# Extra TensorE products with an unread result at three places of a two-layer encoder step, and PSUM buffers dealt out anew in the state-space mixer

## The chip, the cores and the metric

The kernel runs on one core of one Trainium2 chip. The metric is the time of one execution in device microseconds; lower is better. The five engines are named as the profile names them: PE (TensorE's products; PEld is its weight loads), DVE (VectorE), ACT (ScalarE), POOL (GpSimd) and SP (SyncE, which issues most transfers).

## The reference

One inference step of a two-layer encoder over 1024 prompt positions and 64 sample positions, width 1024. Layer 0 mixes with windowed attention, layer 1 with a diagonal state-space model; each layer ends in a gated feed-forward part with a short convolution, and RMS norms stand before and after every part.

```python
def s5_mixer(h, ...):                       # layer 1, 64 groups of 16 channels, 64 complex states each
    lr, li, bbr, bbi = s5_discretize(lam_re, lam_im, log_dt, b_re, b_im)
    ...
        xr = jnp.einsum('blgi,gpi->blgp', u_blk, bbr)
        xi = jnp.einsum('blgi,gpi->blgp', u_blk, bbi)
        ...
        _, _, sr, si = lax.associative_scan(_affine_combine, (ar, ai, xr, xi), axis=1)
        y = jnp.einsum('blgp,gip->blgi', sr, cr) - jnp.einsum('blgp,gip->blgi', si, ci)
    ...
    y = ... + d_skip * h
    z = jax.nn.gelu(y)
    ag = z @ w_glu + b_glu
    return ag[..., :D_MODEL] * jax.nn.sigmoid(ag[..., D_MODEL:]), hr, hi

for i in range(DEPTH):
    x = x + rms_norm(mixer_i(rms_norm(x, g_pre_mix[i])), g_post_mix[i])
    x = x + rms_norm(conv_ffn(rms_norm(x, g_pre_ffn[i])), g_post_ffn[i])
```

## The kernel before

Activations lie with channels on the partitions; the 1088 positions are cut in three blocks (`BLK`: 384, 384 and 320). A big product is done in three passes of fp32r (`mm3`, lines 218 to 222): high part of the weights by low part of the input, high by high, low by high. Weights come one unit of 128x1024 at a time through SP's queue, ACT rounds the high part (L214) and DVE subtracts it (L215).

**The head.** The core starts by loading `x` and the first weight units; `pre_norm` (L281) scales and splits each block on ACT (L288) and DVE (L294), and the first products (L220 to L222, from `attention`) follow as the pieces come. The identity matrix `ident` is made by DVE at L71 in the constructor.

**The norms ahead of the state-space mixer.** When the last block of layer 0's feed-forward part is done, `post_norm` finishes it: sums of squares by products with a column of ones (L254), a root and its reciprocal in a few short DVE steps, the result spread over the partitions by three transposes (L272), then multiplications and additions on DVE (L316, L319). Then `ssm_norm` (L1133) does the same for the norm ahead of the mixer: squares on ACT (L242), sums on DVE (L244, L248), products with ones (L254), the short steps again, and three small products with a selection matrix (L1157). Meanwhile `ssm_bounce` (L1099) writes the block to DRAM and `ssm_load` (L1161) reads it back in another layout as `U`.

**The rounds.** `ssm` (L1179) handles 32 pairs of groups (`q`), 137 columns each (8 positions folded into the rows). `batch` (L1220) takes one or two pairs at a time: 0; 1; then two by two up to 29; 30; 31. These 18 batches run as three stages that overlap (`staged`, L146; the older batch's stage comes first in the program):

- stage 1: TensorE makes the inputs of the scan in the PSUM tile `p1` (L1251, 4 products of 64 weight columns a pair); DVE multiplies them by tables (L1252 and L1255, both read `p1`) and adds (L1256); ACT prepares the tables `sc` and `rd` (L1231, L1234);
- stage 2: DVE scans (L1270) and multiplies by the tables (L1273 makes `gc`, L1274 makes `gs`); ACT copies final states (L1277);
- stage 3: for each pair two PSUM tiles `p3`, `e` = 0 and 1. Each takes one product with the input (L1284, on `U` and `pm`) and four with `gc` and `gs` (L1289, on 64 of the 128 rows: `e` = 0 the upper half, `e` = 1 the lower); ACT copies the two tiles out (L1293). Every fourth pair the copies go to DRAM and come back (L1296, L1301), and ACT applies GELU (L1309, L1312) and rounds (L1318); DVE subtracts (L1322).

All the products named in these stages have plain fp32 operands; the trace shows two records for one such product. The tables `pm` come from DRAM through SP's queue, two transfers a batch of two (L1195). PSUM has eight banks; in this stage they are dealt out as `p1` 2 x 2 banks and `p3` 4 x 1.

After the rounds the gated linear unit begins (`tile_`, L1360), its first product at L220 on `pb`.

**What sets the order.** The program is written for all engines in one sequence; a scheduler reorders it at compile time by its own estimate, and each engine runs its instructions in that fixed order, waiting on semaphores. `order(x, first)` (L112) adds an edge which only the scheduler sees: x is not put before first. A tile pool with a `tag` and `bufs` makes a tile wait for the last reader of the tile that had its buffer.

Of the kernel before, what the change touches and what calls it, by code (L numbers as in the profile page):

```python
# [8 lines left out]
F32 = mybir.dt.float32  # L9
# [6 lines left out]
P = 128  # L16
# [21 lines left out]
NC_ = 137  # L38
# [5 lines left out]
class Core:  # L44
# [173 lines left out]
    def mm3(self, out, w, sl, xh, xl, start, stop):  # L218
# [2 lines left out]
        nc.tensor.matmul(out, w[:, 0, sl], xh, start=False, stop=False)  # L221
        self.last_mm = nc.tensor.matmul(out, w[:, 1, sl], xh, start=False, stop=stop)  # L222


    def rstd(self, src, n, tag, root, bcast=True, first=False, alt=None, adder=None, fine=False):
        nc = self.nc
        adder = adder or nc.vector
        acc = None
        for q in range(4):
            sq = self.n2(n, tag)  # L230
            xq = src[:, 2 * q:2 * q + 2]
            if fine and q == 3:

                adder.tensor_add(acc[:, 0], acc[:, 0], acc[:, 1])
                for j in range(2):
                    nc.scalar.activation(sq[:, j], xq[:, j], AF.Square)
                    adder.tensor_add(acc[:, 0], acc[:, 0], sq[:, j])
                break
            if first:
                nc.gpsimd.tensor_mul(sq, xq, xq)  # L240
            else:
                self.sq[q] = nc.scalar.activation(sq, xq, AF.Square)  # L242
            if q:
                adder.tensor_add(acc, acc, sq)  # L244
            else:
                acc = sq
        else:
            adder.tensor_add(acc[:, 0], acc[:, 0], acc[:, 1])  # L248
        cuts = [min(c, n - P) for c in range(0, n, P)]
        nt = len(cuts)  # L250
        pr = self.sm_ps("pr", int(tag == "sqb") if alt is None else alt)
        st = pr[:, 384:384 + nt]
        for i, c in enumerate(cuts):
            nc.tensor.matmul(st[:, i:i + 1], acc[:, 0, c:c + P], self.ones, start=True, stop=True)  # L254
        v = self.small.tile([P, 4, 4], F32, name="nv" + tag, bufs=3)
        x, hx, r, t = (v[:, i, :nt] for i in range(4))
        if root:
            nc.scalar.activation(x, st, AF.Sqrt, bias=self.eps)
            nc.vector.tensor_scalar(hx, st, 1e-6, -0.5, op0=ALU.add, op1=ALU.mult)
            nc.vector.reciprocal(r, x)  # L260
            self.refine(r, t, hx)
        else:

            nc.vector.tensor_scalar(x, st, 1e-6, None, op0=ALU.add)
            ri = r.bitcast(I32)
            nc.vector.tensor_scalar(ri, x.bitcast(I32), 1, None, op0=ALU.logical_shift_right)
            nc.vector.tensor_scalar(hx, x, -0.5, None, op0=ALU.mult)
            nc.vector.tensor_scalar(ri, ri, -1.0, float(MAGIC), op0=ALU.mult, op1=ALU.add)
            for _ in range(3):
                self.refine(r, t, hx)  # L270
        for i, c in enumerate(cuts if bcast else []):
            nc.tensor.transpose(pr[:, c:c + P], r[:, i:i + 1].to_broadcast([P, P]), self.ident)  # L272
        return pr, r

    def refine(self, r, t, hx):
# [857 lines left out]
    def ssm_norm(self, xt, b):  # L1133

        nc = self.nc
        n = BLK[b][1]
        ps, r = self.rstd(xt, n, "sqa" if b == 2 else "sqb", True, bcast=b < 2, alt=1 - b % 2, adder=nc.gpsimd if b == 0 else None)
        if b == 0:
            jp = self.t4([P, P], "jp", I32)
# [14 lines left out]
        for i, c in enumerate(range(0, n, P)):  # L1154
            c = min(c, n - P) // 8
# [23 lines left out]
    def ssm(self, after):  # L1179
# [4 lines left out]
        with tc.tile_pool(name="ss", bufs=1) as sp:  # L1184
# [2 lines left out]
            self.close_ps()  # L1187
            ps_ctx = tc.tile_pool(name="ps2", bufs=1, space=bass.MemoryType.PSUM)
            ps = ps_ctx.__enter__()

            def load(t, after=None):

# [27 lines left out]
            def batch(qs):  # L1220
# [22 lines left out]
                wk = sp.tile([P, 2, n, 2, 138], F32, name="wk", bufs=3)  # L1243
                A, G = wk[:, 0], wk[:, 1]
                nc.gpsimd.memset(A[:, :, :, 0:1], 0.0)
                p1 = ps.tile([P, 2, 512], F32, name="p1", bufs=2)[:, 0:n, 0:2 * NC_].rearrange("p e (c k) -> p e c k", c=2)
                for i, q in enumerate(qs):
                    for c in range(2):
                        for e, r in enumerate(ROWS):
# [28 lines left out]
                fins.append(x)  # L1278
                yield
                for i, q in enumerate(qs):  # L1280
                    p3 = [ps.tile([P, 512], F32, name="p3", bufs=4)[:, :NC_] for _ in range(2)]
                    for e in range(2):
                        o = OKT + P * e
                        nc.tensor.matmul(p3[e], pm[:, i, o:o + P], U(2 * q + e), start=True, stop=False)  # L1284
                    for c in range(2):
                        for s, g_ in enumerate((gc, gs)):
                            for e, r in enumerate(ROWS):
                                o = OC + P * (c ^ s)
                                nc.tensor.matmul(p3[e], pm[r, i, o:o + P], g_[r, i, c, 0:NC_], start=False, stop=c == 1 and s == 1)  # L1289
                    if q % 4 == 0:  # L1290
                        ys[0] = self.t4([P, 8, NC_], "ys")
                    for e in range(2):
                        out[0] = nc.scalar.activation(ys[0][:, 2 * (q % 4) + e], p3[e], AF.Copy)  # L1293
# [160 lines left out]
def build(tc, a):  # L1454
    nc = tc.nc
    with ExitStack() as ctx:
# [7 lines left out]
        with c.boundary():  # L1464
# [3 lines left out]
            for b in range(3):  # L1468
                step = 2 if b == 0 else 4
                for k in range(0, KD, step):  # L1470
# [4 lines left out]
                    if (b, k) in ((0, 0), (0, 6), (1, 0)):  # L1475
                        c.load_ahead(1 + len(c.ready))
                        c.order(c.loaded, last)
                        last = c.loaded
            c.rest_of_pp()
            for b in range(3):  # L1480
                h.append(c.pre_norm(xt[b], b, g(0), rb, first=b == 0))
# [65 lines left out]
```

## Time and profile before

| | |
|---|---|
| time before, median of 3 runs | 2285.5 us (2285.21 to 2285.83) |
| the profiled execution | 2279.22 us |
| its span, first to last instruction | 2277.4 us |
| PE busy | 2203.5 us (97%) |
| DVE busy | 1683.8 us (74%) |
| ACT busy | 1020.5 us (45%) |
| mean granted clock of TensorE | 0.982 |

A busy share is the time in which the engine had an instruction under way. Matmuls overlap, so the time from one's start to the next one's start tells more than its own length. The granted clock is TensorE's share of 2.4 GHz: 1.00, or 0.50 (1.2 GHz); a value between is a mean over a stretch that has both. In a timeline a line is: start, length, engine, line of the kernel, operation, output and inputs, shapes, count, and in brackets how long the engine sat idle before it and what ended that.

### The profile page before, as it was taken

The numbers are of one execution on the slowest core, as the hardware profiler recorded it, in microseconds if no ns is written. First come the engines' busy times: TensorE is split into PE (matmuls) and PEld (weight loads), VectorE is DVE, ScalarE is ACT, GpSimd is POOL, SyncE is SP. The second block draws the span as 40 slices with busy tenths as digits, with TensorE's granted clock in tenths as the row PEclk, the third lists the DMA queues.
The fourth block names the chain that finished last, engine by engine and source line by source line (L and its number), as shares of the span: only waits on it lengthen the run. The fifth ranks groups of instructions, "written<-read, shape, count | busy, mean of one in ns | idle before, by whom it ended". The sixth has DMA issues, their size and how long they took to land. (4 is left out here: it accounts for less than half of the span.)

```text
span 2277.4 us, 35917 instructions
## 1 busy us (share of the span) xinstructions
PE 2203.5 (97%) x13791; PEld 2126.7 (93%) x13791; DVE 1683.8 (74%) x2954; ACT 1020.5 (45%) x1867; POOL 420.5 (18%) x474
## 2 busy tenths in 40 slices
PE   8999999999999999999978999999999999999997
PEld 7987789999999999999966799999999999999997
DVE  8677648989878776767757845587997787776764
ACT  5255746422333332555544631263444344355543
POOL 6222004100133314001100025452010111110000
PEclk9999999999999999999987889999999999999998
DMA  5100015655245665887749868751265667578773
GB/s 194 36 22 28 20 61 168 236 199 207 91 148 179 194 198 179 278 270 235 241 169 313 227 226 306 277 165 64 95 215 204 239 249 282 183 247 298 230 252 103
DMA packets 208123, 428.46 MB, mean 188 GB/s; under 512 B 23312, under 2 KB 114224, under 8 KB 205008
## 3 DMA queue, kind: packets, MB, share of 16 engines
q1 hardware_dynamic: 175648, 326.56, 43.8%
q0 software_dynamic: 23984, 95.12, 11.5%
q10 hardware_dynamic: 8320, 4.49, 0.8%
q8 instruction: 108, 1.77, 0.3%
q14 instruction: 63, 0.52, 0.1%
HBM read 297.75 MB, written 128.37 MB: 187 GB/s over the span
## 5 line engine op out<-in xcount | busy, mean ns | idle before, releaser
L220 PE MATMUL mm<-hl,whl 128*128 128x384 f32 (+1 forms) x1960 | 645.3, 330 | 15.4 <-ACT whl L214 7.3
L221 PE MATMUL mm<-hh,whl 128*128 128x384 f32 (+1 forms) x1960 | 643.4, 328 | 0.0
L222 PE MATMUL mm<-hh,whl 128*128 128x384 f32 (+1 forms) x1960 | 642.1, 328 | 0.6 <-DVE whl L215 0.6
L220 PEld LDWEIGHTS mm<-hl,whl 128*128 128x128 f32 x1960 | 369.4, 189 | 19.7 <-ACT whl L214 7.3
L214 ACT ACTIVATE whl<-raw 128x1024 fp32r<-128x1024 f32 x202 | 213.0, 1058 | 356.9 <-PE mm L222 157.4
L222 PEld LDWEIGHTS mm<-hh,whl 128*128 128x128 f32 x1960 | 369.1, 188 | 1.4 <-DVE whl L215 1.4
L221 PEld LDWEIGHTS mm<-hh,whl 128*128 128x128 f32 x1960 | 369.5, 189 | 0.0
L215 DVE TENSOR_TENSOR whl<-raw,whl 128x1024 fp32r<-128x1024 f32 x202 | 252.4, 1254 | 105.8 <-ACT whl L214 105.5
L220 PE MATMUL mm<-gt,whl 128*128 128x384 f32 (+1 forms) x968 | 317.0, 328 | 4.0 <-ACT whl L214 1.5
L222 PE MATMUL mm<-gt,whl 128*128 128x384 f32 (+1 forms) x968 | 315.8, 327 | 0.7 <-DVE whl L215 0.7
L221 PE MATMUL mm<-gt,whl 128*128 128x384 f32 (+1 forms) x968 | 316.0, 327 | 0.0
L220 PEld LDWEIGHTS mm<-gt,whl 128*128 128x128 f32 x968 | 181.7, 188 | 5.5 <-ACT whl L214 1.8
L222 PEld LDWEIGHTS mm<-gt,whl 128*128 128x128 f32 x968 | 181.6, 188 | 1.2 <-DVE whl L215 1.2
L221 PEld LDWEIGHTS mm<-gt,whl 128*128 128x128 f32 x968 | 181.7, 188 | 0.0
L194 DVE TENSOR_TENSOR whl<-raw,whl 128x1024 fp32r<-128x1024 f32 x84 | 94.8, 1135 | 69.3 <-ACT whl L193 68.6
L193 ACT ACTIVATE whl<-raw 128x1024 fp32r<-128x1024 f32 x84 | 82.7, 986 | 123.0 <-DMA raw<-sd 56.2
L407 ACT ACTIVATE t<-u,ppt 128x1090 f32<-128x1090 f32 x88 | 114.2, 1298 | 49.3 <-DVE u L509 22.6
L408 DVE SCALAR_TENSOR_TENSOR t<-u,ppt,t 128x1090 f32<-128x1090 f32 x88 | 123.7, 1408 | 9.3 <-ACT t L407 8.7
L409 DVE SCALAR_TENSOR_TENSOR t<-u,ppt,t 128x1090 f32<-128x1090 f32 x88 | 123.5, 1405 | 0.4
L399 DVE TENSOR_TENSOR u<-rb,mm 128x384 f32<-128x384 f32 (+1 forms) x164 | 80.5, 504 | 21.1 <-PE mm L222 16.4
L551 DVE TENSOR_TENSOR gt<-gr,gt 128x768 fp32r<-128x768 f32 (+2 forms) x106 | 90.4, 882 | 6.0 <-ACT gt L550 5.5
L319 POOL TENSOR_TENSOR y<-y,xl 128x768 f32<-128x768 f32 (+1 forms) x16 | 30.6, 1912 | 347.0 <-DVE y L316 283.7
(384 smaller groups left out, 4194.8 us busy)
## 6 DMA issues: line engine op xcount, KB each, us to landing
raw<-in_w_up SPq DMA_DIRECT2D x88, 512.0 KB, 4.2
raw<-in_w_down SPq DMA_DIRECT2D x74, 512.0 KB, 4.5
raw<-sd SPq DMA_DIRECT2D x40, 512.0 KB, 4.3
sj<-in_w_up POOLq DMA_DIRECT2D x68, 256.0 KB, 5.9
su<-sj POOLq DMA_DIRECT2D x34, 512.0 KB, 5.5
raw<-su SPq DMA_DIRECT2D x34, 512.0 KB, 5.0
pm<-prm SPq DMA_DIRECT2D x32, 522.0 KB, 7.1
gr<-td SPq DMA_DIRECT2D x40, 384.0 KB, 5.4
```

The source lines that it names most:

```text
L193: nc.scalar.activation(w[:, 0], raw, AF.Copy)
L194: nc.vector.tensor_sub(w[:, 1], raw, w[:, 0].bitcast(F32))
L214: nc.scalar.activation(w[:, 0], raw, AF.Copy)
L215: nc.vector.tensor_sub(w[:, 1], raw, w[:, 0].bitcast(F32))
L220: nc.tensor.matmul(out, w[:, 0, sl], xl, start=start, stop=False)
L221: nc.tensor.matmul(out, w[:, 0, sl], xh, start=False, stop=False)
L222: self.last_mm = nc.tensor.matmul(out, w[:, 1, sl], xh, start=False, stop=stop)
L399: nc.vector.tensor_mul(u[:, t0 + 2:t0 + 2 + np_], rb[:, t0:t0 + np_], ps[:, :np_])
L407: nc.scalar.activation(t, u[:, 0:T + 2], AF.Identity, bias=cb(m), scale=cw(0, m))
L408: nc.vector.scalar_tensor_tensor(t, u[:, 1:T + 3], cw(1, m), t, op0=ALU.mult, op1=ALU.add)
L409: self.last_conv = nc.vector.scalar_tensor_tensor(t, u[:, 2:T + 4], cw(2, m), t, op0=ALU.mult, op1=ALU.add)
L551: nc.vector.tensor_sub(x[:, 1, u], raw, x[:, 0, u].bitcast(F32))
```

## The change

A new helper `fill` issues products with the identity as weights into a PSUM tile that nothing reads. It is called at three places: at the head, 14 products of 128 columns, as soon as `ident` is there; in `ssm_norm` for the last block, 7 products of 512 columns, put after the last transpose of the `post_norm` before it; and in stage 3 of each of the 18 batches, one product of 384 columns, put after the two L1284 of the batch's first pair and before its first L1289. The moving operand of the wider ones is a part of the constants `pp` that lies in SBUF. To free a bank for the rounds' tile `idle`, `p1` goes from two buffers (2 banks each) to one, and `p3` from four to five.

```diff
--- before.py
+++ after.py
@@ -221,6 +221,15 @@
         nc.tensor.matmul(out, w[:, 0, sl], xh, start=False, stop=False)
         self.last_mm = nc.tensor.matmul(out, w[:, 1, sl], xh, start=False, stop=stop)
 
+    def fill(self, ps, n, cols, first=None):
+
+        for _ in range(n):
+            x = self.nc.tensor.matmul(ps[:, :cols], self.ident, self.pp[:, 64:64 + cols] if cols > P else self.ident[:, :cols], start=True, stop=True)
+            if first is not None:
+                self.order(x, first)
+            first = x
+        return x
+
 
     def rstd(self, src, n, tag, root, bcast=True, first=False, alt=None, adder=None, fine=False):
         nc = self.nc
@@ -269,7 +278,7 @@
             for _ in range(3):
                 self.refine(r, t, hx)
         for i, c in enumerate(cuts if bcast else []):
-            nc.tensor.transpose(pr[:, c:c + P], r[:, i:i + 1].to_broadcast([P, P]), self.ident)
+            self.last_tr = nc.tensor.transpose(pr[:, c:c + P], r[:, i:i + 1].to_broadcast([P, P]), self.ident)
         return pr, r
 
     def refine(self, r, t, hx):
@@ -1134,6 +1143,8 @@
 
         nc = self.nc
         n = BLK[b][1]
+        if b == 2:
+            self.fill(self.mm_ps("idle"), 7, 512, self.last_tr)
         ps, r = self.rstd(xt, n, "sqa" if b == 2 else "sqb", True, bcast=b < 2, alt=1 - b % 2, adder=nc.gpsimd if b == 0 else None)
         if b == 0:
             jp = self.t4([P, P], "jp", I32)
@@ -1187,6 +1198,7 @@
             self.close_ps()
             ps_ctx = tc.tile_pool(name="ps2", bufs=1, space=bass.MemoryType.PSUM)
             ps = ps_ctx.__enter__()
+            idle = ps.tile([P, 512], F32, name="idle")
 
             def load(t, after=None):
 
@@ -1243,7 +1255,7 @@
                 wk = sp.tile([P, 2, n, 2, 138], F32, name="wk", bufs=3)
                 A, G = wk[:, 0], wk[:, 1]
                 nc.gpsimd.memset(A[:, :, :, 0:1], 0.0)
-                p1 = ps.tile([P, 2, 512], F32, name="p1", bufs=2)[:, 0:n, 0:2 * NC_].rearrange("p e (c k) -> p e c k", c=2)
+                p1 = ps.tile([P, 2, 512], F32, name="p1", bufs=1)[:, 0:n, 0:2 * NC_].rearrange("p e (c k) -> p e c k", c=2)
                 for i, q in enumerate(qs):
                     for c in range(2):
                         for e, r in enumerate(ROWS):
@@ -1278,15 +1290,19 @@
                 fins.append(x)
                 yield
                 for i, q in enumerate(qs):
-                    p3 = [ps.tile([P, 512], F32, name="p3", bufs=4)[:, :NC_] for _ in range(2)]
+                    p3 = [ps.tile([P, 512], F32, name="p3", bufs=5)[:, :NC_] for _ in range(2)]
                     for e in range(2):
                         o = OKT + P * e
-                        nc.tensor.matmul(p3[e], pm[:, i, o:o + P], U(2 * q + e), start=True, stop=False)
+                        x = nc.tensor.matmul(p3[e], pm[:, i, o:o + P], U(2 * q + e), start=True, stop=False)
+                    f = self.fill(idle, 1, 384, x) if i == 0 else None
                     for c in range(2):
                         for s, g_ in enumerate((gc, gs)):
                             for e, r in enumerate(ROWS):
                                 o = OC + P * (c ^ s)
-                                nc.tensor.matmul(p3[e], pm[r, i, o:o + P], g_[r, i, c, 0:NC_], start=False, stop=c == 1 and s == 1)
+                                x = nc.tensor.matmul(p3[e], pm[r, i, o:o + P], g_[r, i, c, 0:NC_], start=False, stop=c == 1 and s == 1)
+                                if f is not None:
+                                    self.order(x, f)
+                                    f = None
                     if q % 4 == 0:
                         ys[0] = self.t4([P, 8, NC_], "ys")
                     for e in range(2):
@@ -1476,6 +1492,7 @@
                         c.load_ahead(1 + len(c.ready))
                         c.order(c.loaded, last)
                         last = c.loaded
+            c.fill(c.mm_ps("idle"), 14, P)
             c.rest_of_pp()
             for b in range(3):
                 h.append(c.pre_norm(xt[b], b, g(0), rb, first=b == 0))
```

## Rows read from the trace of the kernel before

**Rows 1.** The page's first table: busy time of each engine, share of the span, instructions.

```profile
PE 2203.5 (97%) x13791; PEld 2126.7 (93%) x13791; DVE 1683.8 (74%) x2954; ACT 1020.5 (45%) x1867; POOL 420.5 (18%) x474
```

**Rows 2.** Stretches of the span, cut where the granted clock changes: start and end in us, length, busy time and count of PE, PEld, DVE, ACT, POOL, then the granted clock, the DMA share and GB/s. The last line is all that follows.

```profile
1183.00:1204.00 21.00, 8.55 (x45) 6.92 (x47) 12.49 (x26) 9.77 (x21) 1.36 (x9) 0.51 0.89 317
...
1214.20:1221.00 6.80, 5.75 (x38) 4.66 (x38) 5.10 (x7) 3.74 (x14) 0.23 (x2) 0.50 1.02 394
1221.00:1241.50 20.50, 17.01 (x195) 13.93 (x194) 18.10 (x25) 12.79 (x41) 1.37 (x9) 1.00 0.89 287
1241.50:1255.20 13.70, 13.70 (x68) 11.18 (x68) 7.61 (x13) 4.95 (x12) 0.66 (x2) 0.50 0.71 224
...
1285.90:1296.10 10.20, 9.59 (x42) 8.06 (x42) 4.53 (x7) 3.06 (x16) 0.29 (x2) 0.50 0.75 237
...
1313.20:1326.90 13.70, 13.00 (x51) 11.15 (x51) 5.59 (x9) 7.10 (x13) 3.40 (x5) 0.50 0.63 186
1326.90:2277.00 950.10, 929.91 (x5638) 924.98 (x5636) 686.62 (x1008) 401.43 (x613) 166.94 (x217) 0.99 0.63 214
```

**Rows 3.** Timeline of DVE in the rounds: starts of L1252, and the L1322 that belongs to every second batch.

```profile
1204.88 0.73 DVE L1252 TENSOR_TENSOR wk<-pm,p 128x548 f32<-128x548 f32 x1 [1.76 <-PE p L1251]
...
1221.70 0.73 DVE L1252 TENSOR_TENSOR wk<-pm,p 128x548 f32<-128x548 f32 x1 [2.23 <-PE p L1251]
...
1227.02 0.72 DVE L1252 TENSOR_TENSOR wk<-pm,p 128x548 f32<-128x548 f32 x1
...
1232.08 0.72 DVE L1252 TENSOR_TENSOR wk<-pm,p 128x548 f32<-128x548 f32 x1
...
1241.61 1.42 DVE L1322 TENSOR_TENSOR zl<-z,zh 128x384 fp32r<-128x384 f32 x3
...
1253.86 0.73 DVE L1252 TENSOR_TENSOR wk<-pm,p 128x548 f32<-128x548 f32 x1 [6.09 <-PE p L1251]
...
1295.75 0.72 DVE L1252 TENSOR_TENSOR wk<-pm,p 128x548 f32<-128x548 f32 x1 [5.47 <-PE p L1289]
```

**Rows 4.** Timeline of PE in the rounds and at the start of the gated linear unit, some of its lines.

```profile
1217.62 1.28 PE L1284 MATMUL p<-U,pm 128*128 128x137 f32 x4
1218.83 2.20 PE L1289 MATMUL p<-wk,pm 64*128 64x137 f32 x16
...
1223.39 0.73 PE L1284 MATMUL p<-U,pm 128*128 128x137 f32 x4
1224.06 1.20 PE L1289 MATMUL p<-wk,pm 64*128 64x137 f32 x16
1225.19 1.62 PE L1251 MATMUL p<-U,pm 128*64 128x137 f32 x24
...
1240.93 0.50 PE L1284 MATMUL p<-U,pm 128*128 128x137 f32 x2 [3.17 <-ACT ys L1293]
...
1246.23 1.28 PE L1284 MATMUL p<-U,pm 128*128 128x137 f32 x4
...
1285.14 0.69 PE L1251 MATMUL p<-U,pm 128*64 128x137 f32 x8 [2.00 <-DMA pm<-prm]
...
1312.49 0.50 PE L1284 MATMUL p<-U,pm 128*128 128x137 f32 x2 [1.94 <-DVE wk L1273]
...
1322.84 0.69 PE L220 MATMUL pb<-zl,whl 128*128 128x384 f32 x1 [0.70 <-ACT ys L1293]
```

**Rows 5.** Timeline of PE in layer 0's feed-forward part: a plain fp32 product of 128 columns (L1050, two records) and an fp32r product of 320 columns by turns.

```profile
653.26 0.38 PE L1050 MATMUL kps<-ct,bd 128*128 128x128 f32 x2
653.40 0.39 PE L221 MATMUL mm<-hh,whl 128*128 128x320 f32 x1
653.62 0.38 PE L1050 MATMUL kps<-ct,bd 128*128 128x128 f32 x2
```

**Rows 6.** Timeline of the head: DVE's identity, the first product, two of the last at the slow pace and two of the first at the fast one, and the place where PE waits for a weight unit that DVE splits.

```profile
1.09 0.23 DVE L71 TENSOR_SCALAR ident<-jp 128x128 f32<-128x128 int32 x1 [0.21 <-POOL jp L97]
...
7.34 0.69 PE L220 MATMUL mm<-hl,whl 128*128 128x384 f32 x1 [7.34 <-ACT whl L214]
...
11.79 0.52 PE L221 MATMUL mm<-hh,whl 128*128 128x384 f32 x1
...
12.11 0.52 PE L222 MATMUL mm<-hh,whl 128*128 128x384 f32 x1
...
12.74 0.34 PE L221 MATMUL mm<-hh,whl 128*128 128x384 f32 x1
...
12.92 0.34 PE L222 MATMUL mm<-hh,whl 128*128 128x384 f32 x1
...
16.52 0.44 PE L222 MATMUL mm<-hh,whl 128*128 128x384 f32 x1 [0.33 <-DVE whl L215]
```

**Rows 7.** Timeline of PE in the norms ahead of the mixer, up to the first product of the rounds.

```profile
1180.87 0.80 PE L254 MATMUL pr<-ones,sqa 128*128 128x1 f32 x6 [1.70 <-DVE sqa L237]
...
1182.89 0.54 PE L272 MATMUL pr<-ident,nvsqa 128*128 128x128 f32 x3 [1.22 <-DVE nvsqa L279]
...
1193.63 1.44 PE L254 MATMUL pr<-ones,sqa 128*128 128x1 f32 x6 [10.20 <-DVE sqa L248]
...
1196.63 1.46 PE L1157 MATMUL pr<-sel 128*128 128x16 f32 x6 [1.56 <-DVE sel L1156]
...
1198.78 1.18 PE L1251 MATMUL p<-U,pm 128*64 128x137 f32 x8 [0.68 <-PE pr L1157]
```

## The prediction

> **What bounds the kernel now.** I read the page's table of engines first: PE is busy in 2203.5 of 2277.4 us [rows 1], so nearly everywhere else the products themselves are the limit and a change can only matter where PE waits or runs slowly. The windows then show where that is [rows 2]: between 1183 and 1327 us the granted clock alternates between 1.00 and 0.50, with half-clock stretches of 21.0, 6.8, 13.7, 10.2 and 13.7 us. These are the norms ahead of the state-space mixer, its rounds, and the first products of the gated unit. After 1326.9 us PE is busy 929.9 of 950.1 us, so what is gained or lost before passes on to the end.
>
> In the rounds, DVE's and PE's timelines are read against each other. At full clock DVE hardly waits: it is busy 18.1 of the 20.5 us from 1221 to 1241.5 [rows 2], and a round of two pairs takes 1232.08 - 1227.02 = 5.06 us of it, plus 1.42 us of L1322 in every second round [rows 3]. At half clock DVE waits for PE: 1.76 us at 1204.88, then 2.23, 6.09 and 5.47 [rows 3]. What PE did before each fall is in its own timeline [rows 4]: it idled 3.17 us before 1240.93 behind ACT, which had not yet copied the `p3` tiles out, and 2.00 us before 1285.14 behind a transfer of `pm`.
>
> **The price of a product that nobody reads.** The trace has none of 384 fp32 columns. The nearest row is L1050, 128 fp32 columns between fp32r products of 320: two of its records and one of the other take 653.62 - 653.26 = 0.36 us, of which the other's share is 0.15 (320/384 of the 0.18 us from one fp32r start to the next, 12.74 to 12.92) [rows 5, 6]. So one such product of 128 columns costs 0.21 us, one of 384 by its columns 0.63, one of 512 0.84. From below, two fp32r records of 384 columns are 0.36 us; from above, L1284 takes 0.67 us for two products of 137 columns (1223.39 to 1224.06) [rows 4], 384/137 of one is 0.94. I take 0.7, near L1050, whose weights are also 128 wide. At half clock L1284 takes 1.21 (1217.62 to 1218.83), 1.8 times as long [rows 4], so 1.26.
>
> **The change part by part, as differences to the span.**
>
> *Head: 0.* The 14 products can start at 1.32, when `ident` is done [rows 6], and cost 14 x 0.21 = 2.9 us at full, 5.3 at half pace. They end by about 7 us, where the first real one starts (7.34); from above, by L1284's price, 14 x 0.31 x 1.8 = 7.9, they would hold it 1.9 us. The real products run 0.32 us apart up to 12.4 and 0.18 after it. A faster pace from 7.34 gains nothing: at 16.52 PE waits for DVE's split of a weight unit [rows 6], and DVE waits for no product before it. That wait also hides a delay of 1.9. If it were gone, the 5.1 us at the slow pace would be worth 5.1 x (1 - 0.18/0.32) = 2.2.
>
> *Norms: -0.6.* The clock falls near 1183 after PE has had only 0.80 and 0.54 us of work since 1179 [rows 7], all before the seven products start at 1183.43; so their beginning is at half pace. They take 7 x 0.84 = 5.9 us at full and 10.6 at half, ending between 1189.3 and 1194.0; the real L254 comes at 1193.63. If the clock is up there, L254 takes 0.80, as at 1180.87, for 1.44: -0.64. L1157 (1.46) could save as much again, but PE idles between, as it did before the fall at 1183. Bounds: -1.3, and +5.6 if all seven cost L1284's upper price at half pace (15.8 us, to 1199.2, past L1157's start at 1196.63 and L1251's at 1198.78).
>
> *Start of the rounds: +0.7.* From 1198.78 to 1204.88 PE works without a gap at half clock [rows 3, 7] and DVE waits. Two products of `fill` now stand in this chain. At full clock the 6.1 us become 3.4 + 1.4 = 4.8: -1.3. At half: +2.5. PE is nearly idle from 1195.1 to 1196.6, so half is likelier; but the clock rises within it, and DVE may be given other work.
>
> *Falls in the rounds: -8.0.* The `fill` stands after the first pair's L1284, where PE next waits for `gc` and `gs`. That helps where PE lacked operands (before 1214), less where L1284 itself is held by `p3`, or L1251 by `pm`: `fill` is behind the stall. What it does in every case is to bind the order. At 1240.93 PE made one `p3` tile's five products and then the other's, 5.30 us for a pair; with both L1284 first, as at 1217.62, 3.4 (half clock), because the products on the two halves of the rows run together [rows 4]. So a fall should last shorter. I count the 2.23 us as gone and half of 6.09 and 5.47: -8.0. Bounds 0 and -13.8.
>
> *Tail: -3.4.* From 1312.49 PE needs 10.35 us at half clock for the last two pairs until the gated unit starts at 1322.84 [rows 4]. With the bound order and two `fill` it is 2 x 3.4 + 2 x 1.26 = 9.3 at half, 2 x 1.80 + 1.4 = 5.0 at full; I take -2.5, a little under the middle. The first 4.06 us of the gated unit, to 1326.9, would be 0.18/0.32 of that at full clock: -1.8, half counted.
>
> *Work added: +1.5.* Eighteen times 0.7 is 12.6 us of PE. A warm round has 16/24 of 1.62 for L1251, twice 1.80 and 0.7: 5.4 us, against DVE's 5.06 and, with L1322, 6.5 [rows 3, 4]. The excess of 0.3 shows in some eight rounds without L1322 (2.4, less what the bound order saves); without DVE as cover all 12.6 would count.
>
> *One `p1` buffer: +1.0.* The next batch's L1251 now waits for L1255 of the present one. Until the next L1252 DVE still has the rest of its 5.06 us, some 3.7 us (5.06 less two of 0.72), for PE's 1.1. Behind the waiting L1251 stand later L1284, and ACT waits for those. The fifth `p3` tile lets one L1284 start early. Bounds 0 and +20 (below).
>
> Sum: 0 - 0.6 + 0.7 - 8.0 - 3.4 + 1.5 + 1.0 = -8.8. It is made on the profiled execution (2279.22, 1.8 above its span, 6.3 under the median); the median shown, 2285.5, becomes **2276.7**.
>
> **The rivals.**
>
> *The clock never falls in the rounds (13%).* For it: warm rounds are nearly full, 5.4 of about 5.8 us. Against: the two stalls lie ahead of `fill`. It gives -0.6 - 1.3 - 13.8 - 5.4 - 1.8 + 2.5 = -20.4: 2265.
>
> *The falls stay as they are (17%).* For it: the stalls of 3.17 and 2.00 us are not touched, and with one `p1` PE can't use them for products of a second batch ahead, as it does at 1225.19 (24 records, a batch and a half). Five `fill` at half pace cost 6.3, four pairs no longer made one tile after the other give back 4 x 1.9 = 7.6, the rest +2.6: 2287, about the same. The Trainium skill, "TensorE: Matmul & The Clock Gate", section "A second HAM failure mode: psum-queue depth-cycling", says that small idles between groups of products, while PE goes round its PSUM banks, keep the clock changing; by that rule a buffer less speaks for this case. The trace agrees as far as the stall before 1240.93 is one for a PSUM tile.
>
> *Slower, by the single `p1` (15%).* If L1251 of the next batch ends after L1274 of the present one, its 1.1 us and a handover of 0.2 come on DVE's path in each of some 16 rounds: up to +20, less 10 for half of the first rival's gain, so 2296. It decides when PE stands behind the present batch's two pairs (3.6 + 0.7 us) at the moment L1255 ends: 3.7 us are left then. Against: these pairs' first products can run earlier. The same page, "Step-by-step: what each phase is for", says that products keep their program order, so that a `fill` ahead would delay L1251; no row here shows one overtaken.
>
> **How the numbers follow.** The main case holds 55%, with 2270 to 2283 as its own range. A measurement of this kernel can tell about 0.2%, 4.6 us. Faster by more: nine tenths of the main case, the first rival, a little of the second, 0.64. Same: 0.19. Slower: 0.17. The range 2262 to 2291 leaves out the far ends of the first and third rival.
>
> **What would show it.** Right: between 1204 and 1327 the half-clock stretches shrink from 6.8 + 13.7 + 10.2 + 13.7 = 44.4 us to under 30, L1289 comes in sixteens at a batch's first pair, and DVE's wait of L1252 for PE falls by about 8 us; the head's 16.52 stays. Wrong: `fill` far from 0.7 us, falls at the same places and as long, L1252 waiting in every round for L1251, or L254 held up by the seven.

## The result, and the profile after

The changed kernel took 2268.99 us at the median of its first four runs (2268.03 to 2273.37) against 2285.36 us of the kernel before: a ratio of 0.9936 (95% interval 0.9918 to 0.9953). Twelve more runs on another occasion (e6_again below) gave 0.9975 (0.9961 to 0.9989). It is faster, by 0.25 to 0.65%; the predicted 2276.7 us lies between the two medians, 2269.0 and 2280.0.

The profiled execution took 2268.03 us, span 2266.3; it is the fastest of the four. PE's row of the page, for the one in [rows 1]:

```profile
PE 2199.2 (97%) x13869; PEld 2119.5 (94%) x13869; DVE 1687.6 (74%) x2954; ACT 1021.7 (45%) x1867; POOL 417.5 (18%) x474
```

The windows, cut where the clock changes, columns as in [rows 2]:

```profile
1193.50:1203.50 10.00, 7.75 (x31) 6.46 (x32) 2.59 (x12) 3.10 (x11) 1.17 (x8) 0.50 1.04 392
1210.50:1214.00 3.50, 3.50 (x34) 3.25 (x32) 2.98 (x4) 3.02 (x10) 0.21 (x2) 0.52 1.03 400
1241.00:1244.50 3.50, 3.50 (x26) 3.00 (x28) 1.79 (x3) 1.34 (x7) 0.00 (x0) 0.52 0.56 209
1268.50:1272.00 3.50, 3.50 (x20) 2.17 (x19) 2.83 (x4) 0.13 (x1) 0.00 (x0) 0.52 1.03 407
1272.00:1313.00 41.00, 34.16 (x354) 26.19 (x353) 34.38 (x52) 31.54 (x84) 2.09 (x11) 1.00 0.76 230
1313.00:1316.50 3.50, 3.17 (x10) 3.17 (x11) 2.58 (x5) 1.23 (x3) 1.66 (x3) 0.53 0.64 178
```

Where the kernel before had half clock for 6.8, 13.7, 10.2 and 13.7 us [rows 2], this one has four falls of about 3.4. (The products' lines move: L254 is now L263, L1157 L1168, L1251 L1263, L1252 L1264, L1273 and L1274 L1285 and L1286, L1284 L1296, L1289 L1302, L1293 L1309, L1309 L1325; L227 is the product of `fill`.) PE's timeline of the rounds:

```profile
1226.01 0.81 PE L227 MATMUL idle<-ppt,ident 128*128 128x384 f32 x2
1226.75 1.21 PE L1302 MATMUL p<-wk,pm 64*128 64x137 f32 x16
...
1239.75 0.50 PE L1296 MATMUL p<-U,pm 128*128 128x137 f32 x2 [3.15 <-ACT ys L1309]
1240.09 0.81 PE L227 MATMUL idle<-ppt,ident 128*128 128x384 f32 x2
...
1268.02 0.50 PE L1296 MATMUL p<-U,pm 128*128 128x137 f32 x2 [3.29 <-ACT ys L1309]
1268.36 1.36 PE L227 MATMUL idle<-ppt,ident 128*128 128x384 f32 x2
1269.64 2.20 PE L1302 MATMUL p<-wk,pm 64*128 64x137 f32 x16
...
1311.43 1.36 PE L1302 MATMUL p<-wk,pm 64*128 64x137 f32 x16 [2.22 <-DVE wk L1285]
1313.33 0.69 PE L220 MATMUL pb<-zl,whl 128*128 128x384 f32 x1 [0.54 <-ACT ys L1309]
```

L1302 comes in sixteens, both `p3` tiles by turns (in two batches as 4 and 28 records). The wait for ACT ahead of L1296 is still there, 3.15 and 3.29 us, and the clock still falls behind it. DVE's waits for PE are of the old kind, only shorter (2.23, 6.09 and 5.47 in [rows 3], 13.8 us together; 0.86, 3.42 and 3.68 here, 8.0), and at the start there is one of 4.39:

```profile
1205.03 0.44 DVE L1264 TENSOR_TENSOR wk<-pm,p 128x274 f32<-128x274 f32 x1 [4.39 <-PE p L1263]
...
1210.81 0.72 DVE L1267 TENSOR_TENSOR wk<-sc,p 128x548 f32<-128x548 f32 x1 [0.56 <-ACT sc L1243]
...
1246.54 0.72 DVE L1264 TENSOR_TENSOR wk<-pm,p 128x548 f32<-128x548 f32 x1 [3.68 <-PE p L1263]
...
1259.01 0.72 DVE L1264 TENSOR_TENSOR wk<-pm,p 128x548 f32<-128x548 f32 x1 [0.86 <-PE p L1263]
...
1274.82 0.73 DVE L1264 TENSOR_TENSOR wk<-pm,p 128x548 f32<-128x548 f32 x1 [3.42 <-PE p L1263]
...
1311.32 0.45 DVE L1286 TENSOR_TENSOR wk<-wk,sc 128x276 f32<-128x276 f32 x1
```

**Where the 11.1 us of the spans came from.** I cut both profiles at four events. The norms' first product is 0.15 us earlier (1180.72 for 1180.87 in [rows 7]); from there to the first product of the rounds both take 17.91 (1198.63 and 1198.78). From that product to the end of DVE's last multiplication (L1286 above, L1274 below) the time falls from 114.88 to 113.14 us, -1.7. From there to the gated unit's first product it falls from 9.18 to 1.56, -7.6; what comes after the gated unit begins gives the last 1.6. So the largest piece is the tail. Here is its beginning in the kernel before, whose gated unit starts at 1322.84 [rows 4]:

```profile
1313.22 0.44 DVE L1274 TENSOR_TENSOR wk<-wk,sc 128x276 f32<-128x276 f32 x1
```

Counted on PE in program order, the kernel before has 48 L1289 (six pairs) behind the last L1251, the changed one 16 (two pairs). With two `p1` the scheduler runs stage 1 ahead to the end of the rounds and stage 3 stays behind; with one it can't. Runs of the same letter on PE, A for L1251, B for L1284, C for L1289, F for `fill`, counts behind them:

```
before: ... A7 B2 C8 B2 C8 B1 C1 B1 C7 B1 C1 B1 C7 B1 C4 B1 C4 B1 C1 B1 C7
after:  ... A8 B2 F1 C8 B2 C8 A4 B2 F1 B3 C16 A4 B1 F1 C8 B2 F1 C8
```

`B1 C4 B1 C4` is one `p3` tile and then the other; the kernel before has this in five pairs (from 1240.93, 1263.78, 1272.01, 1286.52 and 1312.49), the changed one in none. Such a pair is dearer at full clock too: the second of them takes 3.11 us (to 1266.89), one by turns 1.80 (1226.82 to 1228.62).

Four of the six pairs were done at 1310.55. PE then stood still until 1312.49, and the last two pairs made the tail. The profile names L1273 for this wait [rows 4], but L1284 reads nothing of L1273; the weight load of the same product names ACT, which had a GELU and a rounding (from 1308.82 on) ahead of the copies that free `p3`:

```profile
1312.14 0.47 ACT L1293 ACTIVATE ys<-p 128x137 f32<-128x137 f32 x2
```

```profile
1312.49 0.30 PEld L1284 LDWEIGHTS p<-U,pm 128*128 128x128 f32 x2 [2.15 <-ACT ys L1293]
```

In the changed kernel one pair is left there (1311.43). The clock is not what shortens the tail: in e6_again, the same program profiled once more, it took 2.38 us, all of them at half clock:

```profile
1323.54:1325.92 2.38, 1.87 (x17) 1.55 (x15) 2.33 (x5) 1.91 (x9) 0.00 (x0) 0.50 0.14 17
```

### The profile page after: what moved, and what is told of

It is laid out like the page before. It is cut to its first block, busy times and chain, and to the rows that moved or that the text cites. A ratio compares the mean times of both kernels' runs of the same rounds, so it can differ in the third digit from the quotient of the medians.

```text
span 2266.3 us, 36080 instructions
## 1 busy us (share of the span) xinstructions
PE 2199.2 (97%) x13869; PEld 2119.5 (94%) x13869; DVE 1687.6 (74%) x2954; ACT 1021.7 (45%) x1867; POOL 417.5 (18%) x474
## 5 line engine op out<-in xcount | busy, mean ns | idle before, releaser
L215 DVE TENSOR_TENSOR whl<-raw,whl 128x1024 fp32r<-128x1024 f32 x202 | 254.9, 1266 | 95.3 <-ACT whl L214 95.1
L559 ACT ACTIVATE gt<-gr 128x768 fp32r<-128x768 f32 (+2 forms) x106 | 78.3, 772 | 38.3 <-DMA gr<-gd 25.6
```

The lines of the kernel that those rows point to most:

```text
L215: nc.vector.tensor_sub(w[:, 1], raw, w[:, 0].bitcast(F32))
```

## The experiments

Theory A: the order that the product binds (both L1296 ahead of the first L1302) does it. Theory B: the product's own work keeps the clock. Theory C: the single `p1` does it. A rival to all: the products at the head and in the norms. What each run showed, by the same cuts (the last four columns are of one profile each; "rounds" and its clock run from 12 us after the first L1251 to the gated unit, "longest" is the longest half-clock stretch that begins in it, "DVE" the time from the first L1251 to the end of the last L1274, "tail" from there to the gated unit):

| kernel | p1/p3, bound, columns | median (runs) | ratio, 95% | rounds, clock | longest | DVE | tail |
|---|---|---|---|---|---|---|---|
| before | 2/4, no, none | 2282.9 to 2285.4 | 1 | 112.06, 0.82 | 13.7 | 114.9 | 9.2 |
| changed | 1/5, yes, 384 | 2269.0 (4) | 0.9936 (0.9918-0.9953) | 102.70, 0.95 | 3.4 | 113.1 | 1.6 |
| e6_again | the same | 2280.0 (12) | 0.9975 (0.9961-0.9989) | 109.80, 0.89 | 10.2 | 119.4 | 2.4 |
| e1_rounds | 1/5, yes, 384, no ends | 2273.9 (10) | 0.9965 (0.995-0.9981) | 105.01, 0.94 | 6.8 | 114.6 | 2.4 |
| e12_rounds | the same | 2276.9 (12) | 0.9969 (0.9956-0.9983) | 106.81, 0.92 | 6.8 | 117.2 | 1.6 |
| e5_small | 1/5, yes, 16, no ends | 2275.7 (10) | 0.9977 (0.996-0.9995) | 108.27, 0.86 | 6.8 | 117.6 | 2.7 |
| e11_sixteen | the same | 2280.1 (12) | 0.9981 (0.9965-0.9997) | 108.64, 0.86 | 6.8 | 118.0 | 2.7 |
| e10_two | 1/5, yes, 2 x 512, no ends | 2281.6 (12) | 0.9988 (0.9972-1.0003) | 108.30, 1.00 | none | 117.5 | 2.8 |
| e9_bound | 2/4, yes, none | 2279.4 (12) | 0.9979 (0.9965-0.9992) | 109.17, 0.86 | 6.8 | 112.8 | 8.4 |
| e3_deal | 1/5, no, none | 2285.3 (10) | 1.001 (0.9991-1.0028) | 109.48, 0.87 | 13.7 | 118.7 | 2.7 |
| e4_ends | 2/4, no, ends only | 2284.2 (10) | 1.0001 (0.9983-1.0019) | 121.54, 0.77 | 34.1 | 120.4 | 13.1 |
| e7_ahead | 1/5, yes, 384 ahead | 2275.4 (12) | 0.9958 (0.9941-0.9975) | 106.11, 0.92 | 10.2 | 116.5 | 1.6 |
| e8_stall | 1/5, yes, 384 + some | 2280.4 (12) | 0.9984 (0.9967-1.0001) | 109.58, 0.94 | 10.2 | 116.9 | 4.7 |
| e13_gelu | as e12, gelu later | 2280.8 (12) | 0.9985 (0.9971-1.0) | 111.29, 0.92 | 10.2 | 120.2 | 3.1 |

The last four columns scatter as single executions do: the profile of e3_deal is its fastest of ten runs, those of e6_again and e12_rounds are their slowest of twelve. The lines of these kernels are numbered a little differently from the changed kernel's; the tiles and shapes tell which is which (`p<-U,pm` 128\*64 is stage 1, 128\*128 the first product of stage 3, `p<-wk,pm` the ones behind it).

**The ends off, and the ends alone.** e1_rounds and e4_ends.

```diff
# e1_rounds, against the changed kernel
-        if b == 2:
-            self.fill(self.mm_ps("idle"), 7, 512, self.last_tr)
...
-            c.fill(c.mm_ps("idle"), 14, P)
# e4_ends, against the changed kernel: these stay; p1 bufs=2, p3 bufs=4, no idle tile, no fill and no order in stage 3
```

> The changed kernel without the fourteen products at the head and the seven between the norms; the rounds keep the product per batch, its order, the one p1 and the five p3. If the rounds carry the gain: 2269, within 3 us of the changed kernel. If the products at the head or between the norms carry a part of it (the norms' L263 at full pace, a faster start): over 2273.

> The kernel before with only the fourteen products at the head and the seven between the norms. If the rounds carry the gain: 2285, within 3 us of the kernel before, with the half-clock stretches of the rounds as long as before (44 us together or more). If the ends carry it: 2275 or less.

The ends alone are worth nothing that shows (1.0001, within 0.2%), and the rounds without them 0.9965 and 0.9969, at least as good as the 0.9975 of the whole change (e6_again): the gain is in the rounds. The half-clock stretches of e4_ends are even longer than before. The expected "within 3 us of 2269" for e1_rounds was missed by 2, and 2273.9 lies in the other branch, "over 2273". The ratios don't bear that branch out: 2269 was the median of four runs, and the same program's twelve have 2280.0.

**The size of the product: 16, 384, 2 x 512 columns.** e5_small, and once more on one chip e11_sixteen, e12_rounds, e10_two.

```diff
-                    f = self.fill(idle, 1, 384, x) if i == 0 else None
+                    f = self.fill(idle, 1, 16, x) if i == 0 else None     # e5_small, e11_sixteen
+                    f = self.fill(idle, 2, 512, x) if i == 0 else None    # e10_two
```

> The rounds of e1_rounds with the product that nobody reads cut from 384 to 16 columns: the same order of the products, the same PSUM tiles, next to no work. Theory A (the order that the product binds, both L1296 ahead of the first L1302, is what shortens a fall): 2264 to 2271, falls of some 3.4 us each. Theory B (the product's own work keeps PE busy through the wait and so the clock up): falls of 7 to 14 us come back, 2276 to 2284.

> e5_small once more (16 columns for 384), beside e12_rounds on one chip. Theory A: within 2 us of e12_rounds. Theory B: 3 us or more above it, with long falls.

> e1_rounds once more (384 columns), as the middle of the three sizes: a ratio to the kernel before of 0.996 to 0.998, as e1_rounds and e6_again had.

> The rounds alone (no products at the head, none between the norms), with two products of 512 columns in each batch where the changed kernel has one of 384: 2.7 times its work, the same place and the same bound order. Theory B (the product's work keeps the clock up): less half clock in the rounds than e12_rounds, and a time within 3 us of it or below, though it adds 18 x 1.2 us of PE. Theory A (only the order counts): as much half clock, and 3 to 10 us more than e12_rounds, since a warm round of 5.4 us of PE becomes 6.6, as long as DVE's with L1338 and longer than its 5.06 without.

The rounds' windows of e11_sixteen and of e10_two (columns as before), then DVE's and PE's lines of e10_two:

```profile
1213.66:1322.30 108.64, 87.82 (x872) 74.39 (x871) 87.86 (x128) 68.25 (x198) 4.79 (x30) 0.86 0.77 255
```

```profile
1212.44:1320.74 108.30, 99.92 (x897) 69.87 (x896) 88.26 (x127) 67.75 (x194) 4.50 (x30) 1.00 0.84 251
```

```profile
1229.91 1.88 PE L227 MATMUL idle<-ppt,ident 128*128 128x512 f32 x4
1231.72 1.21 PE L1300 MATMUL p<-wk,pm 64*128 64x137 f32 x16
...
1236.31 1.88 PE L227 MATMUL idle<-ppt,ident 128*128 128x512 f32 x4
```

```profile
1235.85 0.72 DVE L1262 TENSOR_TENSOR wk<-pm,p 128x548 f32<-128x548 f32 x1 [2.80 <-PE p L1261]
```

Of the clock theory B is right: in the rounds it is 0.86 at 16 columns (as with the order alone, e9_bound below), 0.89 to 0.95 at 384, and 1.00 at 2 x 512. Of the time the larger part is theory A's: 16 columns have most of the gain (0.9977 and 0.9981), and with the clock never down e10_two is no faster than before within its interval, and its rounds are as long as those with 16 columns. The marks set beforehand are less kind to theory A: e5_small's 2275.7 is over its 2271, with stretches of 6.8 us, and e11_sixteen is 3.2 us over e12_rounds, where theory B had asked for 3. PE now needs 6.40 us for a round (1229.91 to 1236.31) where DVE needs 5.06 without the subtractions [rows 3], and DVE waits for PE at full clock, 2.80 us here. What the clock gives, the product's work takes. 384 columns are in the middle of both: 0.0012 less than 16 columns in either comparison (0.9965 to 0.9977, 0.9969 to 0.9981). The intervals overlap each time, so this advantage of about 2.7 us is likely and not shown. Nor is the order quite the same to the end: 28 products stand behind the last stage-1 product at 16 columns, 16 at 384.

**The order alone, the PSUM tiles alone.** e9_bound and e3_deal.

```diff
# e9_bound, against the kernel before
-                        nc.tensor.matmul(p3[e], pm[:, i, o:o + P], U(2 * q + e), start=True, stop=False)
+                        x = nc.tensor.matmul(p3[e], pm[:, i, o:o + P], U(2 * q + e), start=True, stop=False)
+                    f = x
...
+                                if f is not None:
+                                    self.order(x, f)
+                                    f = None
# e3_deal, against the kernel before: p1 bufs=2 becomes 1, p3 bufs=4 becomes 5
```

> The kernel before, its two p1 and four p3 kept, with only the order bound: in every pair both L1284 ahead of the first of the eight L1289, so that no p3 tile's products run alone. No product that nobody reads. Theory A (tiles one after the other are what makes a fall long): half-clock stretches of the rounds under 30 us for 44, and 2270 to 2276. Theory B (the product's work is needed): the long stretches stay, 2280 to 2286.

> The kernel before with one p1 and five p3 and nothing else: no product that nobody reads, no edge. The order that comes out has eight L1263 together ahead of every batch's first L1296, but three batches near the end run the two p3 tiles one after the other. Theory C (the one p1, which makes every round alike, carries the gain): 2268 to 2274. Theory A (the bound order carries it): 2276 to 2284, with the long falls where tiles run one after the other. The prediction's third rival (the one p1 costs in every round): over 2290.

The order by itself (bound in every pair), with no product and the old tiles, gives 0.9979, about 5 us. The 2279.4 lie between theory A's 2270 to 2276 and theory B's 2280 to 2286. The longest half-clock stretch is 6.8 us for 13.7, as theory A says, though the sum, 37.5 us for 44.4, did not get under the 30 I had asked. DVE's waits for PE in its rounds are 3.6 us for 13.8, the least of all. But DVE waits more for ACT instead (11.9 us over its run, 4.6 in the kernel before), so the run is only 2.1 us shorter, and the tail stays:

```profile
1315.47 0.44 DVE L1283 TENSOR_TENSOR wk<-wk,sc 128x276 f32<-128x276 f32 x1
```

```profile
1324.31 0.69 PE L220 MATMUL pb<-zl,whl 128*128 128x384 f32 x1 [4.34 <-ACT ys L1306]
```

Half of this tail is not PE's: its last pair ended at 1319.97, and then it waited 4.34 us for ACT, which ran a GELU and two roundings ahead of the last two copies. In e8_stall below, 3.06 of the tail's 4.7 us are the same.

```profile
1319.56 2.03 ACT L1322 ACTIVATE z<-yf 128x1024 f32<-128x1024 f32 x1 [1.19 <-DMA yf<-yd]
...
1323.83 0.43 ACT L1306 ACTIVATE ys<-p 128x137 f32<-128x137 f32 x2
```

The tiles by themselves are the mirror image: tail 2.7 us (28 L1289 behind the last stage-1 product, not 48), DVE's run 3.9 us longer, median 2.4 us above the kernel before with an interval that holds 1. Four of its pairs still run tile after tile, and PE waits 7.60 us for ACT once, which itself had waited 5.61 us for the transfer of `yf`:

```profile
1246.61 0.82 PE L1293 MATMUL p<-U,pm 128*128 128x137 f32 x2 [7.60 <-ACT ys L1302]
```

So theory C alone falls: the new tiles shorten the tail and give it back in DVE's run. It is not given back as waits for PE, which are 16.3 us over the run for 18.1 before. DVE has two more weight splits of the gated unit ahead of the cut (L215, five for three, 2.4 us), and it waits 4.6 us for ACT ahead of one subtraction (1.9 in all before). Nor does a run show that the tiles add anything to the bound order: with both and 16 columns the ratio is 0.9977 and 0.9981, with the order alone 0.9979. One `p1` and the fifth `p3` were not tried apart.

**The product at other places.** e6_again is the changed kernel for comparison; e7_ahead puts the product ahead of the first L1296; e8_stall adds two products there in the batches that wait.

```diff
# last_a[0] is the last L1263 issued
+                    g = self.fill(idle, 1, 384, last_a[0]) if i == 0 else None                                       # e7_ahead
+                    g = self.fill(idle, 2, 512, last_a[0]) if i == 0 and qs[0] > 5 and qs[0] % 4 == 2 else None      # e8_stall
...
+                        if g is not None:
+                            self.order(x, g)
-                    f = self.fill(idle, 1, 384, x) if i == 0 else None     # e7_ahead only
+                    f = x if i == 0 else None
```

> The changed kernel once more, unedited, beside the next three. Its first four runs had a ratio of 0.9936 to the kernel before; e1_rounds, which lacks the products at the head and between the norms, had 0.9965, and e4_ends, which has them alone, 1.0001. If the ends are worth nothing, this comes out between 0.994 and 0.9975; if they add to the rounds, at 0.9945 or less.

> The changed kernel with the product that nobody reads moved in each round: ahead of the first L1296 instead of behind the second, so that it can run in the wait for the p3 tiles; both L1296 still stand ahead of the first L1302. The prediction's reason why falls stay (the product stands behind the wait) says: idles ahead of L1296 shrink from 3.2 to 2.4 us, some falls vanish, 2 to 5 us less than the changed kernel. If only the product's work within a round counts, wherever it stands: the same as the changed kernel within 3 us. If it delays L1263 of the batch after and so DVE: 2 to 5 us more.

> The changed kernel with two more products of 512 columns ahead of the first L1296 of each batch that waits for ACT behind a gelu (the batches whose idle was 3.15, 1.55, 3.29, 1.64 and 1.45 us). By 0.73 us for 384 columns two of 512 fill 1.9 us of such an idle. If the idle causes the falls: the falls of 3.4 us after 1240 and 1268 vanish, no half clock between 1214 and 1310, 3 to 6 us less than the changed kernel. If the falls come by something else: they stay, and the time is 0 to 4 us more.

e7_ahead has the lowest ratio of the runs beside it, 0.9958, 4.6 us under e6_again, but the intervals meet, and the reason expected is not what its profile shows: it still has a wait of 6.33 us and a half-clock stretch of 10.2 behind it.

```profile
1236.32 0.91 PE L227 MATMUL idle<-ppt,ident 128*128 128x384 f32 x2
1237.07 0.40 PE L1297 MATMUL p<-U,pm 128*128 128x137 f32 x2
1243.79 0.82 PE L1297 MATMUL p<-U,pm 128*128 128x137 f32 x2 [6.33 <-ACT ys L1312]
```

e8_stall did most of what it was made for (the falls that the changed kernel has at 1241 and 1268.5 are gone) and gained nothing. Its windows:

```profile
1219.00:1287.50 68.50, 63.59 (x612) 46.69 (x610) 59.92 (x85) 42.15 (x127) 3.17 (x21) 1.00 0.86 281
1287.50:1294.00 6.50, 6.21 (x30) 4.63 (x32) 1.75 (x3) 2.69 (x13) 0.00 (x0) 0.50 0.58 203
```

No fall for 68.5 us; then ACT was later than the two products are long, and the clock fell:

```profile
1282.13 1.98 PE L227 MATMUL idle<-ppt,ident 128*128 128x512 f32 x4
1283.95 0.40 PE L1297 MATMUL p<-U,pm 128*128 128x137 f32 x2
1287.79 0.83 PE L1297 MATMUL p<-U,pm 128*128 128x137 f32 x2 [3.44 <-ACT ys L1312]
```

In the stretch without falls DVE still waited for PE four times, 0.77 to 1.60 us, and the ratio, 0.9984, is no better than e6_again's. Waits filled this way kept the clock and gave no time.

**ACT's wait.** e13_gelu. What holds the copies of `p3` is ACT's own order. Ahead of the wait of 3.29 us at 1268.02 it stood 2.17 us for the transfer of `yf`, then ran the GELU, the rounding and the next tables, and copied `p3` at 1267.69:

```profile
1261.18 2.06 ACT L1325 ACTIVATE z<-yf 128x1024 f32<-128x1024 f32 x1 [2.17 <-DMA yf<-yd]
```

e13_gelu is e12_rounds with each GELU but the last two one step of the schedule later.

```diff
                     if kt < 7:
                         yield
                         yield
+                        if kt < 6:
+                            yield
```

> e12_rounds with each gelu but the last two one step of the schedule later, so that ACT finds its yf tile loaded and does not hold the copies of p3 behind that transfer. If ACT's wait for the transfer is a large part of the idle ahead of L1296: idles of 3.2 us become 2 or less, fewer falls, 3 to 8 us less than e12_rounds. If the scheduler only moves the wait (the gelus meet later copies, or pile up ahead of the gated unit): the same time or up to 5 us more.

The scheduler moved the wait, and the median is 3.9 us above e12_rounds, which the second branch allows; the intervals overlap. ACT now waited for the copies' way to DRAM, 4.60 us at the longest, and PE behind it (ACT's line, then PE's):

```profile
1248.33 2.03 ACT L1325 ACTIVATE z<-yf 128x1024 f32<-128x1024 f32 x1 [4.60 <-DMA yd<-ys]
```

```profile
1251.96 0.82 PE L1294 MATMUL p<-U,pm 128*128 128x137 f32 x2 [6.00 <-ACT ys L1307]
```

Also not tried: the bound order with two `p1` in the rounds (e9_bound's short DVE run) and one at the end (the short tail). The cuts suggest it; no run shows it.

## Why the prediction was right, and where its terms were not

The sum said -8.8, the spans of the first profiles -11.1, the two ratios -15 and -6 us of 2285. The time and the direction are right, the distribution over the terms is not, and the closeness of the number is in part luck.

- **Price: right.** 1226.75 - 1226.01 = 0.74 us at full and 1269.64 - 1268.36 = 1.28 at half clock for the estimated 0.7 and 1.26; 0.90 for 512 columns in e10_two (half of 1229.91 to 1231.72) for 0.84.
- **Head, 0: right.** The fourteen took 5.37 us, as much as the 5.3 reckoned for half pace alone. The first real product came 0.37 later than 7.34, and the wait for the split stays, at 16.99.

```profile
1.38 5.37 PE L227 MATMUL idle<-ident 128*128 128x128 f32 x28 [1.38 <-DVE ident L71]
7.71 0.44 PE L220 MATMUL mm<-hl,whl 128*128 128x384 f32 x1 [0.97 <-ACT whl L214]
...
16.99 0.44 PE L222 MATMUL mm<-hh,whl 128*128 128x384 f32 x1 [0.33 <-DVE whl L215]
```

- **Norms, -0.6: too much.** The seven took 7.87 us and raised the clock on the way, as said. But PE then idled 2.50 us for DVE, and the clock was falling again when L263 came: 1.44 us, as before [rows 7].

```profile
1183.12 7.87 PE L227 MATMUL idle<-ppt,ident 128*128 128x512 f32 x14
1193.48 1.44 PE L263 MATMUL pr<-ones,sqa 128*128 128x1 f32 x6 [2.50 <-DVE sqa L257]
```

In e4_ends, e6_again, e7_ahead and e8_stall the same line took 0.89, 0.95, 1.17 and 1.44; the mean gain over the five is 0.26 us. The step that failed is "if the clock is up there": I let PE's work end at 1189 to 1194 and did not count the idle behind it.
- **Start, +0.7: right.** Both products ran near half clock ahead of the second batch's L1264, which waited 4.39 us; DVE's L1267 of the third batch came at 1210.81, 12.18 us after the first L1263; in the kernel before the same step is at 1209.97, 11.19 after it. That is +1.0.
- **Falls in the rounds, -8.0: mechanism right, size wrong.** The falls became shorter with the bound order (the longest 6.8 without any product, 3.4 to 10.2 with one of 384 columns, 13.7 and more without the order), the wait ahead of L1296 stayed, and the half clock of the rounds fell from 44.4 to four times 3.4, 13.6 us (27.3 in e6_again), under the 30 I had named. But DVE's waits for PE fell by 5.8, not 8, and DVE's run as a whole by only 1.7; over the four profiles with 384 columns it is 1.2 longer at the mean (113.1, 119.4, 114.6, 117.2).
- **One `p1`, +1.0: not to be told apart.** e3_deal's DVE run is 3.9 longer, e5_small's and e11_sixteen's 2.9 at the mean, but some 2.4 of it are the weight splits that moved ahead of the cut. The third rival's mechanism, DVE waiting for L1263 behind the present batch's pairs, does not show in the sum: over the run DVE waits for PE 13.3 us in the changed kernel, 16.3 in e3_deal and 18.1 in the kernel before. No kernel with one `p1` came near its 2296; the slowest, e3_deal, has 2285.3.
- **Tail, -3.4: too small, and for the wrong reason.** It was -7.6 up to the gated unit (-2.5 forecast), and -6.1 to -7.6 in every kernel with one `p1` but e8_stall (-4.5). I priced the same two pairs at a better clock. In fact one of them no longer stands there: with the new tiles the scheduler interleaves stage 3 earlier, and two pairs for six are left behind the last stage-1 product. The clock has little part in it, as the 2.38 us at half clock show. The order on PE in the kernel before (24 records of L1251 ahead at 1225.19 [rows 4]) was a hint at this.
- **Work added, +1.5: right at one product** (a round takes 1231.34 - 1226.01 = 5.33 us for the 5.4 expected), and e10_two shows the other bound.

```profile
1231.34 0.81 PE L227 MATMUL idle<-ppt,ident 128*128 128x384 f32 x2
```

The first rival, a clock that never falls, did not come to pass at 384 columns. It did at 2 x 512, with 2281.6 and not near its 2265, but with 2.7 times the product's work, for which it had no term. The second, falls as they are, is what e3_deal shows (13.7), without the order. The rule of the Trainium skill, "TensorE: Matmul & The Clock Gate", section "A second HAM failure mode: psum-queue depth-cycling", is borne out as far as it goes: two of the four falls in the changed kernel's rounds, 1241 and 1268.5, followed a wait of 3.15 and 3.29 us for a PSUM tile. The other two came after idles of 2.16 and 2.22 us of another kind. The Trainium skill, on the same page, section "Step-by-step: what each phase is for", says that products keep program order, and e7_ahead's lines above agree, where the product ran first and L1297 waited behind it.

So two errors cancelled. For DVE's run (start, falls, work and `p1`) the terms gave +0.7 - 8.0 + 1.5 + 1.0 = -4.8; it was -1.7 in the first profile and +1.2 at the mean of four. For the tail they gave -2.5; it was -7.6, and -7.2 at the same mean. Some 2.4 us of the difference are only the cut, which the two weight splits crossed. Run and tail together were to give -7.3 and gave -9.4, and -6.0 at the mean of four.

## What to carry to other kernels

An unread product has three effects, its work, the order that it binds and the buffers that it takes, and each is to be priced and tried alone: here the order alone gave about 5 us and adds no work to PE. A better granted clock is no gain in itself where the filler's columns make PE's round longer than that of the engine that bounds it. And when a buffer count changes, read the compiled order up to the end of the stage: what is left behind the last dependent step (six pairs, then two) moved the tail by 6 us and more in most profiles here. But add up all pieces before you call it a gain: alone, the new tiles shortened the tail by 6.4 us and the time by nothing.

## What the runs showed of the hardware

Two profiles of the identical program differ by more than the change is worth. In e6_again the norms began 5.98 us later than in the first profile of the changed kernel (1186.70 for 1180.72), before anything of the rounds. Part of it are falls that the other profile does not have, in stretches that are nearly full of products. The same windows of e6_again and of the first profile:

```profile
858.50:862.00 3.50, 2.91 (x13) 2.43 (x12) 3.47 (x8) 1.92 (x5) 1.94 (x2) 0.53 0.10 42
1118.00:1121.50 3.50, 3.50 (x15) 3.50 (x15) 1.05 (x1) 1.02 (x2) 0.00 (x0) 0.52 0.73 235
```

```profile
858.50:862.00 3.50, 3.50 (x22) 3.50 (x23) 3.18 (x5) 1.97 (x4) 2.66 (x2) 1.00 0.93 299
1118.00:1121.50 3.50, 3.50 (x27) 3.49 (x26) 3.11 (x4) 2.65 (x6) 0.89 (x1) 1.00 0.63 184
```

What follows the start of the gated unit, which no experiment touched, took 948 to 959 us from profile to profile. This is why medians of ten runs still leave 0.15%, and why I read stages by cuts and not by spans.

Second, PE without a gap is not PE at full clock. In the kernel before, the stretch from 1241.5 to 1255.2 is at 0.50 with PE busy throughout [rows 2]. The tiles one after the other, which I took for its cause, end in the middle of it, at 1246.23; the products by turns behind them ran at half clock too:

```profile
1246.23 1.28 PE L1284 MATMUL p<-U,pm 128*128 128x137 f32 x4
1247.44 2.20 PE L1289 MATMUL p<-wk,pm 64*128 64x137 f32 x16
```

Of the half-clock stretches that began more than 12 us into the rounds, the longest was 10.2 us in the eleven profiles with the bound order, and 13.7, 13.7 and 34.1 in the three without. So the order goes with shorter falls; what ends one stays open.
